# Four seven-product blocks and one plain unit in each feed-forward layer, in place of three and three

## The chip, the cores and the metric

The kernel runs on one NeuronCore of a Trainium2 chip. The metric is device time in microseconds (us) of one launch, from device measurement; the number before is the median of three runs. TensorE (PE) multiplies, VectorE (DVE), ScalarE (ACT) and GpSimd (POOL) prepare operands and read results, SyncE (SP) issues most of the transfers from device memory. [...]

## What is computed

An encoder trunk for 256 tokens of width 1024, two layers deep. Each layer is feed-forward, mixer, feed-forward, each with a residual and a layer norm; the mixer is an mLSTM in the first layer and a windowed attention in the second. The change touches the four feed-forward layers (FFNs):

```python
def swiglu(x, w_in, w_out):                 # x 256 x 1024, w_in 1024 x 5632, w_out 2816 x 1024
    gu = x @ w_in
    g, u = gu[..., :D_FF], gu[..., D_FF:]   # D_FF = 2816
    return (jax.nn.silu(g) * u) @ w_out

x = layer_norm(ALPHA * x + 0.5 * swiglu(x, ffn_w_in[l, 0], ffn_w_out[l, 0]), ...)
```

All of it is in 32-bit floats. TensorE multiplies a shorter format, so each operand is split into a high part (`_hi`, a rounded copy) and a low part (`_lo`, the operand less its high part), and one product is three matmuls: high by high, high by low, low by high (`mm3`).

## The kernel before

The weights are read once, in pieces ("words") of 128 x 1024 numbers, 512 KB each. The order in which the words are used is a list, the plan, made before anything is emitted. Each entry of the plan is one *split*: ACT writes `w_hi` (a cast), then DVE writes `w_lo` (a subtraction). At most `RING` = 10 splits exist ahead of TensorE. Raw words of kind `w_raw` have four buffers for the whole program and two more in an FFN (`v_raw`); words of kind `s_raw` have six buffers, which exist only inside an FFN and are opened at its start (`W.open`). All loads go through SP's queue in program order; transfers that add to what stands in SBUF go through POOL's.

The intermediate width 2816 of an FFN is worked off in blocks of columns:

- the **head**: 512 gate and 512 up columns by plain products, 8 splits, 96 matmuls of 128 x 512;
- then `GROUPS` = 3 times a **unit** and a **seven**. A unit is 256 gate and 256 up columns by plain products: 4 splits, 48 matmuls. A seven is 512 gate and 512 up columns by seven half-size products instead of eight (a Strassen-Winograd scheme): 14 splits, 84 matmuls instead of 96.

The seven takes x in four quarters (token half t, half of the 1024 inputs): A11, A12 for t = 0, A21, A22 for t = 1, and the weights in four quarters: B11, B21 (gate columns, upper and lower rows), B12, B22 (up columns). Each quarter of weights is two words. The products, named P1 to P7 here in the order of the plan, are

| product | x side | weight side | how the weight side is made |
|---|---|---|---|
| P1 | A11 | B11 | as loaded |
| P2 | A12 | B21 | as loaded |
| P3 | S1 = A21 - A22 | B11 + B12 | DVE adds, in place, after P1's split |
| P4 | S2 = S1 - A11 | + B22 | DVE adds, in place, after P3's split |
| P5 | S3 = A11 - A21 | B12 + B22 | DVE adds, in place |
| P6 | S4 = A12 + S2 | B22 | as loaded |
| P7 | A22 | P4's weights + B21 | transfer adds, in place, after P4's split |

So B11's two words are split three times with sums between the splits, and each such sum and split depends on the one before. The four sums of x, S1 to S4, are made and split once per FFN (`x_one`, `x_two`, `x_rest`); before the change they read `xr`, a copy of x that `x_raw` puts together from the high and low parts of the transposed x.

Between the products lie the **downs**, rows of `w_out` times finished columns of the hidden layer: `down(1)` is one split and 12 matmuls into four accumulators (`py`). A seven has four downs (after P2, P4, P6, P7; the last seven has two), a unit two, and six are left for the end (the tail), beside which the layer norm runs. Finished hidden columns are transposed by TensorE (`tr`), then split by ACT and DVE into `h_hi`, `h_lo`; `b_mul` makes the head's hidden columns `hh`.

A small model of the engines' clocks inside the program (`Paced`) decides where among the instructions the next cast, subtraction or sum is put. In the rows of the profile nearly every compute instruction has the line L134, since one helper records them all; groups are told apart by the names of their tiles: `w_lo<-s_raw` is a split of a seven's word, `w_lo<-w_raw` of any other word, `s_raw<-s_raw` a sum of weights by DVE, `S` and `S_lo` the sums of x, `py` matmuls are downs, `pw` matmuls everything else.

Of the kernel before, what the change touches and what calls it, by code (L numbers as in the profile page):

```python
# [12 lines left out]
OP = mybir.AluOpType  # L13
# [10 lines left out]
GROUPS = 3  # L24
# [292 lines left out]
def trunk_kernel(ctx: ExitStack, tc: tile.TileContext, x, ffn_w_in, ffn_w_out, ln_g, ln_b, ml_w_in, ml_gate_b,  # L317
# [42 lines left out]
    def seven(w, c0, c1, downs):  # L360

        at = lambda r0, c: [two(w, r0 + 256 * j, c) for j in range(2)]
        b12, b11, b22 = ([word(x, 2, "s_raw") for x in at(*p)] for p in ((0, c1), (0, c0), (512, c1)))
# [3 lines left out]
        for j in range(2):  # L367
            after[s1[j]] = [(b11[j], b12[j])]
        downs(0)
# [7 lines left out]
        [split_of(w_, None, p) for w_, p in zip(b12, s6)]  # L377
# [7 lines left out]
    for j, (kind, l, i, _) in enumerate(stages):  # L385
        if kind == "ffn":
# [112 lines left out]
    def to_xT(t, src, bank, halves=range(2)):  # L499
        for h in halves:  # L500
# [3 lines left out]
            split_evac(pair(xT, A, slice(4 * h, 4 * h + 4), tok(t)), p)  # L504

    def warm(n):

        p = ybank((128, 4, 128))
        for j in range(n):
            nc.tensor.transpose(p[:, j % 4], ident, ident)  # L510
# [64 lines left out]
    def ffn(l, i, n, pending, last):  # L575
        with ExitStack() as ph:
# [47 lines left out]
            xr = [pool.tile([128, 8, 128], F32, name=f"xr{t}", tag="h" + e, bufs=2) for t, e in enumerate(("_hi", "_lo"))]  # L624
            xs = {}
# [12 lines left out]
            low, high = slice(0, 4), slice(4, 8)  # L638
            f1 = {}
# [14 lines left out]
            if start:  # L654
                sg = {}
                for m in range(2):
                    ps = [wbank(), wbank()]
                    for a in range(4):
# [7 lines left out]
                        early = {2: lambda: x_raw(0), 3: lambda: x_raw(1), 4: x_one, 5: x_two, 6: x_rest}  # L666
# [7 lines left out]
            else:  # L674
                W.open(pool, ends[bound[0]])
                for t in range(2):
                    ps = [wbank(), wbank()]
                    for m in range(2):
                        for a in range(4):
# [5 lines left out]
                            if t == 1 and a % 2:  # L685
                                [[None, lambda: x_raw(0), None, lambda: x_raw(1)], [None, x_one, None, x_two]][m][a]()
# [675 lines left out]
```

## Time and profile before

| | |
|---|---|
| median of three runs | 942.7 us (942.70, 942.92, 941.75) |
| span of the profiled execution, first to last instruction | 941.2 us; no time of that execution beside its span is given, the three times lie 0.6 to 1.7 us above it |
| TensorE busy | 98% of the span, 4416 matmuls, granted clock 0.998 |
| VectorE busy | 85%, 943 instructions |
| ScalarE busy | 58% |
| GpSimd busy | 11% |
| transfers | 187.54 MB, mean 199 GB/s |

Order of the stages in the span: FFN 0 from the start to about 190 us, mLSTM, FFN 1 from about 300 us, FFN 2 from about 481 us, attention, FFN 3 from about 755 us. Busy shares are those of the profiler: the ends of matmuls are modelled, so the share of TensorE tells that it always has something in flight, not that it is at its peak; starts are exact.

### The profile page before, as it was taken

The numbers are of one execution on the slowest core, as the hardware profiler recorded it, in microseconds if no ns is written. First come the engines' busy times: TensorE is split into PE (matmuls) and PEld (weight loads), VectorE is DVE, ScalarE is ACT, GpSimd is POOL, SyncE is SP. The second block draws the span as 40 slices with busy tenths as digits, with TensorE's granted clock in tenths as the row PEclk, the third lists the DMA queues.
The fourth block names the chain that finished last, engine by engine and source line by source line (L and its number), as shares of the span: only waits on it lengthen the run. The fifth ranks groups of instructions, "written<-read, shape, count | busy, mean of one in ns | idle before, by whom it ended". The sixth has DMA issues, their size and how long they took to land.

```text
span 941.2 us, 12338 instructions
## 1 busy us (share of the span) xinstructions
PE 925.3 (98%) x4416; PEld 766.4 (81%) x4416; DVE 800.0 (85%) x943; ACT 546.5 (58%) x781; POOL 103.2 (11%) x162
## 2 busy tenths in 40 slices
PE   9999999999999999999999999999999999999996
PEld 7788888889878787888888888887887788888885
DVE  6899997787697889988888899977878888898975
ACT  5656756347563548565535566563678554757460
POOL 0030101011111000101010101010544300000100
PEclk9999999999999999999999999999999999999999
DMA  7969773646534949685549597746543266769531
GB/s 267 358 154 338 209 265 75 216 134 204 177 108 145 314 150 327 173 327 134 180 155 338 132 324 210 249 90 200 175 147 104 68 215 254 229 219 306 162 91 45
DMA packets 98461, 187.54 MB, mean 199 GB/s; under 512 B 6720, under 2 KB 37456, under 8 KB 98400
## 3 DMA queue, kind: packets, MB, share of 16 engines
q1 hardware_dynamic: 91072, 173.04, 53.1%
q0 software_dynamic: 6752, 12.66, 8.4%
q10 hardware_dynamic: 576, 1.05, 0.3%
q8 instruction: 35, 0.57, 0.2%
q14 instruction: 26, 0.21, 0.1%
HBM read 185.68 MB, written 1.05 MB: 198 GB/s over the span
## 4 chain that ended last, share of the span: by engine, by line
PE 73%; DVE 12%; DMA 6%; ACT 4%; issue 3%; POOL 1%; SPq 0%; DVEq 0%; ACTq 0%
PE pw L134 46%; PE py L134 27%; DVE w_lo L134 5%; DMA w_raw<-in_ffn_w_in_dram 3%; ACT w_hi L134 2%; DMA w_raw<-in_ffn_w_out_dram 1%; DVE s_raw L134 1%; DMA s_raw<-in_ffn_w_in_dram 1%; ACT sc L134 1%; DVE h L134 1%; DVE o L134 1%; DVE e L134 1%; DMA w_raw<-in_ml_w_in_dram 0%; DVE pr_lo L134 0%; ACT xT_hi L134 0%
## 5 line engine op out<-in xcount | busy, mean ns | idle before, releaser
L134 DVE TENSOR_TENSOR w_lo<-w_raw,w_hi 128x1024 fp32r<-128x1024 f32 (+1 forms) x237 | 280.9, 1216 | 16.0 <-ACT w_hi L134 14.0
L134 ACT CAST w_hi<-w_raw 128x1024 fp32r<-128x1024 f32 (+1 forms) x237 | 240.4, 1049 | 75.4 <-DMA w_raw<-in_ffn_w_out_dram 21.7
L134 PE MATMUL pw<-w_hi,xT_hi 128*128 128x512 f32 x560 | 222.6, 397 | 0.2 <-ACT xT_hi L134 0.2
L134 PE MATMUL pw<-w_hi,xT_lo 128*128 128x512 f32 x560 | 218.9, 391 | 0.2 <-DVE xT_lo L134 0.2
L134 PE MATMUL pw<-w_lo,xT_hi 128*128 128x512 f32 x560 | 218.3, 390 | 0.2 <-DVE w_lo L134 0.2
L134 ACT CAST w_hi<-s_raw 128x1024 fp32r<-128x1024 f32 x144 | 148.4, 1052 | 94.1 <-DVE s_raw L134 58.3
L134 DVE TENSOR_TENSOR w_lo<-s_raw,w_hi 128x1024 fp32r<-128x1024 f32 x144 | 172.6, 1219 | 19.2 <-ACT w_hi L134 19.1
L134 PE MATMUL py<-w_hi,h_hi 128*128 128x512 f32 x352 | 138.2, 393 | 0.3 <-ACT h_hi L134 0.3
L134 PE MATMUL py<-w_hi,h_lo 128*128 128x512 f32 x352 | 137.4, 390 | 0.2 <-DVE h_lo L134 0.2
L134 PE MATMUL py<-w_lo,h_hi 128*128 128x512 f32 x352 | 137.1, 390 | 0.2 <-DVE w_lo L134 0.2
L134 PEld LDWEIGHTS pw<-w_hi,xT_lo 128*128 128x128 f32 x560 | 105.1, 188 | 23.7 <-DVE xT_lo L134 1.0
L134 PEld LDWEIGHTS pw<-w_lo,xT_hi 128*128 128x128 f32 x560 | 105.4, 188 | 21.3 <-DVE w_lo L134 0.9
L134 PEld LDWEIGHTS pw<-w_hi,xT_hi 128*128 128x128 f32 x560 | 105.3, 188 | 21.0 <-ACT xT_hi L134 1.0
L134 DVE TENSOR_TENSOR s_raw<-s_raw 128x1024 f32<-128x1024 f32 x72 | 87.0, 1219 | 0.6
L263 POOL DMA_DIRECT2D s_raw<-in_ffn_w_in_dram x24 | 29.2, 1215 | 496.9 <-DVE w_lo L134 378.7
L134 PEld LDWEIGHTS py<-w_hi,h_lo 128*128 128x128 f32 x352 | 66.1, 188 | 15.2 <-DVE h_lo L134 1.4
L134 PEld LDWEIGHTS py<-w_lo,h_hi 128*128 128x128 f32 x352 | 66.1, 188 | 13.9 <-DVE w_lo L134 0.6
L134 PEld LDWEIGHTS py<-w_hi,h_hi 128*128 128x128 f32 x352 | 66.1, 188 | 13.9 <-ACT h_hi L134 0.7
L134 PE MATMUL pw<-w_hi,S_hi 128*128 128x512 f32 x192 | 74.7, 389 | 0.0
L134 PE MATMUL pw<-w_hi,S_lo 128*128 128x512 f32 x192 | 74.7, 389 | 0.0
L134 PE MATMUL pw<-w_lo,S_hi 128*128 128x512 f32 x192 | 74.7, 389 | 0.0
L134 DVE TENSOR_TENSOR h_lo<-pw,h_hi 128x512 fp32r<-128x512 f32 x44 | 30.1, 687 | 24.5 <-ACT h_hi L134 24.4
(218 smaller groups left out, 1118.1 us busy)
## 6 DMA issues: line engine op xcount, KB each, us to landing
w_raw<-in_ffn_w_out_dram SPq DMA_DIRECT2D x88, 512.0 KB, 5.3
s_raw<-in_ffn_w_in_dram SPq DMA_DIRECT2D x72, 512.0 KB, 6.1
w_raw<-in_ffn_w_in_dram SPq DMA_DIRECT2D x56, 512.0 KB, 5.2
w_raw<-in_ffn_w_in_dram SPq DMA_DIRECT2D x96, 256.0 KB, 4.7
s_raw<-in_ffn_w_in_dram POOLq DMA_DIRECT2D x24, 512.0 KB, 6.1
w_raw<-in_ml_w_in_dram SPq DMA_DIRECT2D x24, 512.0 KB, 4.6
w_raw<-in_at_w_in_dram SPq DMA_DIRECT2D x12, 512.0 KB, 3.8
w_raw<-in_ml_w_out_dram SPq DMA_DIRECT2D x8, 512.0 KB, 3.8
```

What stands on the lines that cost most here:

```text
L134: r = f(out, *args, **kw)
L263: nc.gpsimd.dma_start(t.rearrange("p (k f) -> p k f", k=self.words[w]["k"]), v, accum_op=OP.add)
```

## The change

Each FFN becomes: head, seven, seven, unit, seven, seven, tail. The order is now a list, `PARTS`, with the number of downs at each place; the first three sevens have four downs, the last has two, the unit has two and the tail six, as before. Three further edits come with it. The second of the two words of B12 + B22 (P5's weights) gets its B22 by an adding transfer from device memory (`BY_DMA = (1,)`), issued after the first sum, instead of by DVE. The sums of x read the transposed x where TensorE left it in PSUM (`xp`), and one quarter, A21, is first copied to SBUF by ACT (`x_copy`); `xr` and `x_raw` are gone, and in FFNs 1 to 3 all of the sums now come inside the head. The list of words has B11 ahead of B12. `warm` takes its PSUM bank from the other pool.

```diff
-GROUPS = 3
+PARTS = [("s", (1, 1, 1, 1)), ("s", (1, 1, 1, 1)), ("u", 2), ("s", (1, 1, 1, 1)), ("s", (1, 1, 0, 0))]
+TAIL = 6
+BY_DMA = (1,)
...
     def seven(w, c0, c1, downs):
-        b12, b11, b22 = ([word(x, 2, "s_raw") for x in at(*p)] for p in ((0, c1), (0, c0), (512, c1)))
+        b11, b12, b22 = ([word(x, 2, "s_raw") for x in at(*p)] for p in ((0, c0), (0, c1), (512, c1)))
...
-        for j in range(2):
+        t3 = [None, None]
+        for j, a in enumerate(at(512, c1)):
             after[s1[j]] = [(b11[j], b12[j])]
+            if j in BY_DMA:
+                after[s1[j]].append((b12[j], a))
+                t3[j] = s1[j]
...
         for j, a in enumerate(at(512, c0)):
-            after[s6[j]] = [(b11[j], a), (b12[j], b22[j])]
+            after[s6[j]] = [(b11[j], a)]
+            if j not in BY_DMA:
+                after[s6[j]].append((b12[j], b22[j]))
+                t3[j] = s6[j]
...
-            for g in range(GROUPS):
-                c0 = 512 + 768 * g
-                for a in range(4):
-                    beside(wi, a * 256, c0, F + c0)
-                down(2)
-                seven(wi, c0 + 256, F + c0 + 256, lambda i_: down(1) if g < GROUPS - 1 or i_ < 2 else None)
-            down(6)
+            c0 = 512
+            for what, n_ in PARTS:
+                if what == "u":
+                    for a in range(4):
+                        beside(wi, a * 256, c0, F + c0)
+                    down(n_)
+                    c0 += 256
+                else:
+                    seven(wi, c0, F + c0, lambda i_, n_=n_: down(n_[i_]))
+                    c0 += 512
+            down(TAIL)
...
             split_evac(pair(xT, A, slice(4 * h, 4 * h + 4), tok(t)), p)
+            xp[t, h] = p
...
-            def x_raw(t):
-                nc.vector.tensor_add(xr[t], xT[0][:, :, tok(t)].bitcast(F32), xT[1][:, :, tok(t)].bitcast(F32))
...
+            def x_copy():
+                f1["a21"] = temp("a21").rearrange("p (k m) -> p k m", k=4)
+                nc.scalar.copy(f1["a21"], xp[1, 0])
             def x_one():
-                f1["S1"] = x_sum("S1", xr[1][:, low], OP.subtract, xr[1][:, high])
+                f1["S1"] = x_sum("S1", f1["a21"], OP.subtract, xp[1, 1])
             def x_two():
-                f1["S2"] = x_sum("S2", f1["S1"], OP.subtract, xr[0][:, low])
+                f1["S2"] = x_sum("S2", f1["S1"], OP.subtract, xp[0, 0])
             def x_rest():
-                x_sum("S4", xr[0][:, high], OP.add, f1["S2"])
-                x_sum("S3", xr[0][:, low], OP.subtract, xr[1][:, low])
+                x_sum("S3", xp[0, 0], OP.subtract, f1["a21"])
+                x_sum("S4", xp[0, 1], OP.add, f1["S2"])
...
-                                [[None, lambda: x_raw(0), None, lambda: x_raw(1)], [None, x_one, None, x_two]][m][a]()
+                                [[None, x_copy, None, x_one], [None, x_two, None, x_rest]][m][a]()
...
-                if g == 0 and not start:
-                    x_rest()
-                turn = seven(g < GROUPS - 1, unit_turn)
+            turns = [lambda t=t: tr(hB0, t, hs[t]) for t in range(0 if start else 1, 2)]
+            for g, (what, n_) in enumerate(PARTS):
+                if what == "u":
+                    turns = [unit(turns)]
+                    down(n_)
+                else:
+                    turns = [seven(n_, turns)]
```

In the changed program TensorE has 4368 matmuls instead of 4416, and POOL issues 48 adding transfers of 512 KB instead of 24. The transposes of the head's last hidden columns, which stood in the middle of the first unit, stand right behind P1 of the first seven.

More of the change, by code (lines that the diff above doesn't have):

```diff
@@ L722, in copied, with seven @@
                 return e
-            def seven(full, unit_turn):
+            def seven(downs, turns):
                 of = lambda k0, t: (lambda k: pair(xT, A, k0 + k, tok(t)))
@@ L758, in seven @@
                 product(qa, of(0, 0), True, end1)
-                unit_turn()
+                for f in turns:
+                    f()
                 product(qc, of(4, 0), True, end2)
-                down(1)
+                down(downs[0])
                 qb = wbank()
@@ L764, in seven, with unit @@
                 product(qa, sum_("S2"), False, end6)
-                down(1)
+                down(downs[1])
                 product(qa, sum_("S3"), False, end7)
                 product(qb, sum_("S4"), False, end3)
-                if full:
-                    down(1)
+                if downs[2]:
+                    down(downs[2])
                     tr(hB, 0, v["u0"])
                 product(qa, of(4, 1), False, end4)
-                if full:
-                    down(1)
-                else:
+                if not downs[2]:
                     tr(hB, 0, v["u0"])
+                down(downs[3])
                 return lambda: tr(hB, 1, v["u1"])
-            turn = None
-            for g in range(GROUPS):
+            def unit(turns):
                 ps = [wbank(), wbank()]
@@ L788, in ffn @@
                     if a == 1:
[L789 to L793 removed]
+                        for f in turns:
+                            f()
                 hh = []
```

28 lines of the change are left out of this document (11 added, 17 removed).

## The prediction

> **What bounds the kernel now.** I read the page first: the span, then busy time and the transfer queues.
>
> ```profile
> span 941.2 us, 12338 instructions
> ...
> PE 925.3 (98%) x4416; PEld 766.4 (81%) x4416; DVE 800.0 (85%) x943; ACT 546.5 (58%) x781; POOL 103.2 (11%) x162
> ...
> q1 hardware_dynamic: 91072, 173.04, 53.1%
> q0 software_dynamic: 6752, 12.66, 8.4%
> ...
> s_raw<-in_ffn_w_in_dram POOLq DMA_DIRECT2D x24, 512.0 KB, 6.1
> w_raw<-in_ml_w_in_dram SPq DMA_DIRECT2D x24, 512.0 KB, 4.6
> ```
>
> TensorE is busy 98% of the span, VectorE 85%. The waits of TensorE, longest first, then tell whether the 98% hides starvation:
>
> ```profile
> PE py L134 <- DVE ident L134: 1.4, 1, 1.4
> ```
>
> The longest wait in total is 1.4 us. So TensorE sets the time, and a matmul that goes is a gain in full, provided that the split weights still come in time. What one costs is read from the chain of waits in order of time, in the steady part of FFN 2 (start, length, what):
>
> ```profile
> 515.79 5.44 PE py L134 x24
> ...
> 535.30 2.72 PE py L134 x12
> ...
> 563.49 5.44 PE py L134 x24
> ```
>
> 24 matmuls take 5.44 us, 226.7 ns each. The rows at 515.79 and 563.49 are both the downs of a unit, so 47.7 us is one unit and one seven. The table by stretches has VectorE's share of that period:
>
> ```profile
> 515.79:563.49 47.70, 47.70 (x218) 39.39 (x217) 43.94 (x46) 30.50 (x38) 2.42 (x2) 1.00 0.72 226
> ```
>
> VectorE works 43.94 of 47.70 us: it is the next bound, 8% behind. Its groups in two such periods (count, then busy us and mean ns):
>
> ```profile
> L134 DVE TENSOR_TENSOR s_raw<-s_raw 128x1024 f32<-128x1024 f32 x16 | 19.4, 1220 | 0.2
> L134 DVE TENSOR_TENSOR h_lo<-pw,h_hi 128x512 fp32r<-128x512 f32 x6 | 4.1, 686 | 0.7 <-ACT h_hi L134 0.7
> L134 DVE TENSOR_TENSOR e<-e,pw 128x512 f32<-128x512 f32 x4 | 2.7, 680 | 0.0
> ```
>
> **The steady balance.** Back to back, a DVE instruction on 1024 columns takes less than its 1.22 us: starts lie 1.14 us apart (503.80 and 504.94 below). By the same difference an instruction on 512 takes 0.61. A seven with four downs is 84 + 48 matmuls, 29.9 us, and eight transposes, about 0.9 us: 30.8 us. For it VectorE now does 18 splits, 6 sums, 5 steps on products and 2 `h_lo`: 24 x 1.14 + 7 x 0.61 = 31.6 us. A unit with two downs is 72 matmuls and four transposes, 16.8 us; VectorE needs 6 x 1.14 + 0.75 + 0.61 = 8.2 us. So VectorE falls a little behind in every seven and earns 8 us in every unit, and today a unit stands ahead of each seven.
>
> **The change part by part.**
>
> *Matmuls.* Per FFN two units (96) go and one seven (84) comes: 12 fewer, 48 in all, 48 x 0.2267 = 10.9 us less. Transposes and downs stay in number. This is the whole gain, as TensorE is the bound: 942.7 - 10.9 = 931.8 if nothing waits.
>
> *VectorE's work.* Per FFN six splits come (6.8 us), 20 sums stand where 18 did (2.3), two `x_raw` additions go (2.3), steps on products and `h_lo` grow by about 1.5: 8 us more per FFN, 800 to about 833 us. A mean of 87% isn't a bound; the order is.
>
> *Half of P5's sum by transfer.* One DVE sum per seven goes: 30.5 us instead of 31.6, just under TensorE's 30.8. POOL issues 24 more adding transfers; its row gives 6.1 us to landing. The transfer starts after the first two sums, P5's second split comes six splits and four sums later, about 11 us, so 5 us of cover. POOL's queue holds behind it only the next such transfers and, in FFN 0, small loads for the mLSTM. Cost nothing; if a landing came 5 us later than that, TensorE would wait for the excess.
>
> *Sums of x from PSUM.* Two DVE additions (2.3 us) go, one ACT copy of 512 columns comes, on an engine 58% busy. The steps read PSUM at 680 ns (`e<-e,pw`) and SBUF at 680 (the `S` row below): no price. [...] The four `py` banks are held until the last sum; the first down comes after P2, later than that sum, so nothing waits for the banks.
>
> *The start of each FFN.* Here I expect the loss. In FFN 2 of the trace (start, length; DVE):
>
> ```profile
> 487.84 1.22 DVE L134 TENSOR_TENSOR w_lo<-w_raw,w_hi 128x1024 fp32r<-128x1024 f32 x1
> ...
> 503.80 1.23 DVE L134 TENSOR_TENSOR w_lo<-s_raw,w_hi 128x1024 fp32r<-128x1024 f32 x1 [0.52 <-ACT w_hi L134]
> 504.94 0.68 DVE L134 TENSOR_TENSOR S<-xr 128x512 f32<-128x512 f32 x1
> 506.31 0.69 DVE L134 TENSOR_TENSOR S_lo<-S,S_hi 128x512 fp32r<-128x512 f32 x1 [0.69 <-ACT S_hi L134]
> ...
> 517.31 0.75 DVE L134 TENSOR_TENSOR hh<-sg,pw 128x256 f32<-128x256 f32 x2 [0.32 <-ACT sg L134]
> ...
> 531.70 1.22 DVE L134 TENSOR_TENSOR w_lo<-w_raw,w_hi 128x1024 fp32r<-128x1024 f32 x1
> ```
>
> The first split of P1 ends at 505.02 (503.80 + 1.22); the split of the down after P4 ends at 532.92. VectorE takes 27.9 us for that stretch. It holds all four sums of x, each with a 0.69 us wait for ACT's cast, and for the unit only the `hh` pair (0.75 + 0.32 idle) and one `h_lo` with its wait, about 0.9. Without the unit it is 26 us. TensorE's way over the same stretch is from 521.23 (515.79 + 5.44) to 535.30: 14.1 us. So VectorE must have P1's first split 12 us ahead of its use. Today it has 16, since unit and downs lie between. After the change P1 follows the head at once. The head ends where the unit's first matmul starts:
>
> ```profile
> 504.28 0.39 PE L134 MATMUL pw<-w_hi,xT_hi 128*128 128x512 f32 x1
> ```
>
> At 504.3 + 14.1 = 518.4 TensorE would want the down after P4. When can VectorE have it? The loads decide, in SP's order:
>
> ```profile
> 489.08 1.20 SPq L98 DMA_DIRECT2D w_raw<-in_ffn_w_in_dram  x2
> 491.42 1.48 SPq L100 DMA_DIRECT2D w_raw<-in_ffn_w_out_dram  x2
> 493.00 2.86 SPq L100 DMA_DIRECT2D s_raw<-in_ffn_w_in_dram  x4
> ```
>
> ```profile
> DMA to landing us min/median/max: 6.9/9.1/11.3
> ```
>
> A seven's words are loaded behind the second of the first two downs' words, and in the changed program too. That one waits for a `w_raw` buffer, which the head's eighth split frees (487.84 + 1.22 = 489.06); the unit's words at 489.08 and one more `w_raw` are no longer ahead. So B11 is asked for at about 489.6 instead of 493.0. If its landing takes the 6.9 us of the quickest one in this stretch, it is there at 496.5; with the 4.6 us of the page's last row above, loads of the same size with less ahead of them, at 494.2. The split itself, a cast about as long as the subtraction's 1.22 and the subtraction, adds 2.3, so P1's first split ends between 496.5 and 498.8, and the down after P4 is split 26 us later, 522.5 to 524.8. TensorE waits 4.1 to 6.4 us in this FFN. I take 4.6, near the lower end, since fewer loads are queued ahead than in the trace. Part of it should stand behind P1, where the transposes of `hh` wait: `hh` now follows all sums of x on DVE's queue.
>
> FFN 3 has the same order: 4.6 us. FFN 1 too, with slower loads at its start:
>
> ```profile
> 312.99 7.68 DMA s_raw<-in_ffn_w_in_dram
> ```
>
> 7.7 us instead of 6.9: I take 4.6 here too. FFN 0 makes the sums of x earlier:
>
> ```profile
> 26.61 2.35 DVE L134 TENSOR_TENSOR w_lo<-w_raw,w_hi 128x1024 fp32r<-128x1024 f32 x2
> ...
> 42.89 1.22 DVE L134 TENSOR_TENSOR w_lo<-s_raw,w_hi 128x1024 fp32r<-128x1024 f32 x1
> ...
> 62.59 1.22 DVE L134 TENSOR_TENSOR w_lo<-w_raw,w_hi 128x1024 fp32r<-128x1024 f32 x1
> ```
>
> ```profile
> 31.19 0.39 PE L134 MATMUL pw<-w_hi,xT_hi 128*128 128x512 f32 x1
> ```
>
> There the stretch takes 63.81 - 44.11 = 19.7 us, and P1's first split can't come before the head's eighth split (about 27.8, the first of the pair at 26.61), two remaining sums of x (4 x 0.61 + 2 x 0.69), one `hh` and itself: 33.4. So the down after P4 is split at 53 or later; TensorE wants it at 31.2 + 14.1 + 0.4 = 45.7, a wait of 7.4. I take 6.4, since without `x_raw` the eighth split may come earlier; if the remaining sums too are done before it, 3.8 us go and 2.6 are left.
>
> *The second seven.* It follows without a unit. At 30.5 against 30.8 us VectorE gains nothing on it, and inside a seven it needs its lead, since the sums fall between P1 and P5. I take 1 us per FFN, between 0 and 2.5. From the unit on VectorE has some 8 us of lead, and the rest runs as now.
>
> **The sum.** 4.6 x 3 + 6.4 + 4 x 1 = 24.2 us of waits, less 10.9: 13.3 us more. On the profiled span 941.2 becomes 954.5; the median lies 1.5 us above the span, so 956. With the low ends (4.1 x 3 + 2.6 + 0) it is 947, with the high ends (6.4 x 3 + 7.4 + 10) 968; hardly all at once, so 947 to 966 for this case.
>
> **Rivals.**
>
> *The lead holds: faster.* If B11 lands early enough for P1's first split to be done by 492.4 (518.4 - 26) in FFN 2 and correspondingly elsewhere, TensorE never waits, and the time is 931.8. It breaks even at 2.7 us of waits per FFN, a split done by 495.1. For it: the six `s_raw` buffers are free early and SP could ask sooner than I think; VectorE's 26 us holds waits that shrink when it is late. Against: the landing rows, and that today's lead of 16.2 us at P1 (505.02 against 521.23) is down to 2.4 at the down after P4 (532.92 against 535.30). 931.8 to 941, chance 0.22. That it comes out within 0.2% (about 2 us, what a measurement of this kernel can tell from no change) is the edge between the cases: 0.05.
>
> *Transfers become the bound: slower still.* By the queue rows a 512 KB load takes 53.1% of 941.2 us over 330 such loads, 1.51 us of all 16 engines, and an adding transfer 8.4% over 24, 3.3 us. Two sevens need 24 of the one and 6 of the other, 56 us, against 61.6 of TensorE. If the adding ones grew by half when three fall in one seven, it would be 66, 4 us over in each FFN: 956 + 17 = 973. [...] Against: today's share stays at 0.72 in the steady period above, and words are asked for 10 us ahead. Chance 0.07.
>
> **How the numbers follow.** Forecast 956, chance 0.66. Slower in all 0.66 + 0.07 = 0.73, same 0.05, faster 0.22. The range reaches down into the faster case to 936, leaving about 0.1 below, and up to 966, leaving 0.09 above.
>
> **What the profile after would show.** Right: 4368 matmuls; VectorE near 830 us busy; waits of TensorE for `w_lo`, `h_lo` or the transposed `hh` of several us in each of the four first sevens, none after the unit; the stretch from P1 to the down after P4 some 5 us longer than 14.1. Wrong: TensorE's starts without gaps there (then the loads came earlier, or VectorE needed less than 26 us), or gaps in the third and fourth sevens (then the balance of the unit is wrong).

## The result, and the profile after

| | us, median | ratio to before (95% interval) |
|---|---|---|
| before (run beside it) | 942.33 | |
| after | 1005.93 | 1.0674 (1.0655 to 1.0694) |
| forecast | 956, 936 to 966 | |

The change costs 63.6 us; 13 were forecast. The page of the kernel after, by the same lines as before:

```profile
span 1003.0 us, 12342 instructions
...
PE 937.7 (93%) x4368; PEld 764.2 (76%) x4368; DVE 836.1 (83%) x971; ACT 576.0 (57%) x813; POOL 132.3 (13%) x186
...
q1 hardware_dynamic: 82368, 173.04, 48.9%
q0 software_dynamic: 13280, 25.25, 15.4%
...
s_raw<-in_ffn_w_in_dram POOLq DMA_DIRECT2D x48, 512.0 KB, 6.0
```

The work is as forecast: 4368 matmuls and VectorE 836 us busy (forecast some 830). But TensorE is busy 93% instead of 98%. Its waits, longest in total first (us in total, times, longest):

```profile
PE pw L136 <- DVE w_lo L136: 18.5, 22, 2.2
PE pw L136 <- DVE hh L136: 18.3, 3, 9.0
PE py L136 <- DVE w_lo L136: 7.8, 8, 1.8
PE py L136 <- DVE h_lo L136: 4.9, 3, 2.0
```

Before, the longest total here was 1.4 us. In every one of these rows TensorE waits for VectorE. Where, the table by stretches tells. These are the blocks of FFN 2, each from its first matmul to the next block's: head, first seven, second seven, unit, third seven, fourth seven, tail. (Columns: length; busy us and count of PE, PEld, DVE, ACT and POOL; granted clock; share and rate of transfers.)

```profile
513.46:537.90 24.44, 23.72 (x109) 19.09 (x108) 17.74 (x22) 11.65 (x16) 1.46 (x1) 1.00 0.83 296
537.90:577.30 39.40, 33.41 (x141) 26.44 (x140) 34.03 (x37) 23.17 (x28) 3.64 (x3) 0.96 0.60 176
577.30:610.33 33.03, 31.63 (x141) 25.40 (x140) 30.85 (x31) 21.24 (x25) 3.62 (x3) 1.00 0.85 244
610.33:627.14 16.81, 16.81 (x77) 13.90 (x76) 15.78 (x16) 9.87 (x12) 1.20 (x1) 1.00 0.83 286
627.14:658.02 30.88, 30.88 (x141) 25.55 (x140) 28.79 (x30) 19.78 (x24) 2.41 (x2) 1.00 0.82 244
658.02:684.76 26.74, 25.68 (x117) 20.97 (x116) 19.47 (x19) 16.02 (x19) 3.61 (x3) 1.00 0.53 124
684.76:708.49 23.73, 20.03 (x85) 15.52 (x84) 20.39 (x24) 9.97 (x13) 1.46 (x1) 0.93 0.51 177
```

The last seven and the tail of FFN 2 in the kernel before:

```profile
616.66:642.08 25.42, 25.42 (x117) 21.06 (x116) 20.68 (x21) 18.10 (x21) 1.20 (x1) 1.00 0.52 135
642.08:660.68 18.60, 18.31 (x85) 14.57 (x84) 13.12 (x18) 4.94 (x8) 1.46 (x1) 1.00 0.54 178
```

A seven at full pace takes 30.9 us, the last one 25.4, as they did before; a unit takes 16.8. The unit and the third seven run at full pace, the first seven takes 8.5 us more, the second 2.2, the fourth 1.3, and the tail 5.1 more than the 18.6 of before. The other layers, from starts read in the same way:

| us more than full pace (tail and head: than before) | FFN 0 | FFN 1 | FFN 2 | FFN 3 | sum | forecast |
|---|---|---|---|---|---|---|
| head | 2.5 | -0.7 | 1.2 | 0.3 | 3.3 | with the next |
| first seven | 5.3 | 11.3 | 8.5 | 8.7 | 33.8 | 20.2 |
| second seven | 3.3 | 2.2 | 2.2 | 2.1 | 9.8 | 4 |
| unit, third seven | 0 | 0 | 0 | 0 | 0 | 0 |
| fourth seven and tail | 6.9 | 9.1 | 6.4 | 5.4 | 27.8 | 0 |

74.7 us in all, less 10.9 of matmuls and less 2.7 that the blocks of before had lost themselves, is 61.1; the spans differ by 61.8.

**The first seven.** TensorE in FFN 2 (start, length, what, and in brackets the wait before it and for whom):

```profile
545.19 1.09 PE L136 MATMUL pw<-ident,hh 128*128 128x128 f32 x4 [4.63 <-DVE hh L136]
...
546.51 0.63 PE L136 MATMUL pw<-w_lo,xT_hi 128*128 128x512 f32 x1
546.93 0.63 PE L136 MATMUL pw<-w_hi,xT_lo 128*128 128x512 f32 x1
```

```profile
545.10:548.00 2.90, 2.81 (x9) 2.46 (x10) 2.15 (x3) 1.53 (x2) 0.00 (x0) 0.50 0.00 0
548.00:551.00 3.00, 3.00 (x13) 2.42 (x13) 1.68 (x3) 1.05 (x1) 1.21 (x1) 0.95 0.00 0
```

After P1 TensorE stands for 4.63 us until `hh` is there, and then works at about half pace: matmuls start 0.42 us apart instead of 0.23. The second view, by stretches, says why: the clock granted from 545.1 to 548.0 is 0.50. VectorE in the same stretch:

```profile
528.61 0.69 DVE L136 TENSOR_TENSOR xT_lo<-py,xT_hi 128x512 fp32r<-128x512 f32 x1 [3.91 <-ACT xT_hi L136]
...
529.82 2.35 DVE L136 TENSOR_TENSOR w_lo<-s_raw,w_hi 128x1024 fp32r<-128x1024 f32 x2
...
558.88 1.22 DVE L136 TENSOR_TENSOR w_lo<-w_raw,w_hi 128x1024 fp32r<-128x1024 f32 x1
```

P1's first split ends at 531.04 (the first of the pair at 529.82), the split of the down after P4 at 560.10 (558.88 + 1.22). That is 29.1 us where I had reckoned 26. The row at 528.61 is `xT_lo`, which waited 3.91 us for ScalarE and stands ahead of that split. ScalarE was late with its `xT_hi` (done at 528.58) because the cast of B11's first word stands ahead of it and waited for its load:

```profile
527.05 1.05 ACT L136 CAST w_hi<-s_raw 128x1024 fp32r<-128x1024 f32 x1 [3.07 <-DMA s_raw<-in_ffn_w_in_dram]
```

So the late landing of B11 delays P1's split twice, by the word itself and by `xT_lo`. B11's loads on SP's queue (start, time in which they were issued, count):

```profile
517.18 4.42 SPq L102 DMA_DIRECT2D w_raw<-in_ffn_w_out_dram  x2
522.51 3.38 SPq L102 DMA_DIRECT2D s_raw<-in_ffn_w_in_dram  x6
```

The loads of two downs, which wait for buffers, take until 521.60; the seven's words follow at 522.51, 9.05 us after the layer's first matmul.

**The end.** VectorE and TensorE at P7's second word and in the tail of FFN 2:

```profile
677.50 0.69 DVE L136 TENSOR_TENSOR e<-e,pw 128x512 f32<-128x512 f32 x1 [2.13 <-PE pw L136]
680.22 0.69 DVE L136 TENSOR_TENSOR e<-pw,e 128x512 f32<-128x512 f32 x1 [2.03 <-PE pw L136]
...
681.56 1.22 DVE L136 TENSOR_TENSOR w_lo<-s_raw,w_hi 128x1024 fp32r<-128x1024 f32 x1
```

```profile
682.83 0.50 PE L136 MATMUL pw<-w_lo,xT_hi 128*128 128x512 f32 x1 [1.06 <-DVE w_lo L136]
...
687.40 0.49 PE L136 MATMUL py<-w_lo,h_hi 128*128 128x512 f32 x1 [1.77 <-DVE w_lo L136]
...
700.89 0.50 PE L136 MATMUL py<-w_hi,h_lo 128*128 128x512 f32 x1 [1.75 <-DVE h_lo L136]
```

The split of P7's second word (681.56) stands behind three steps on products, and the first two wait 2.13 and 2.03 us for TensorE. It is ready at 682.78, TensorE uses it at 682.83: its lead, the time for which a split is ready before TensorE uses it, is down to 0.05 us. From there the tail's words come one by one, just in time, and then this follows on ScalarE:

```profile
692.43 1.05 ACT L136 CAST w_hi<-w_raw 128x1024 fp32r<-128x1024 f32 x1 [4.23 <-DMA w_raw<-in_at_w_in_dram]
...
697.57 0.58 ACT L136 CAST h_hi<-pw 128x512 fp32r<-128x512 f32 x1
```

The cast `h_hi` of the last seven's second half stands in ScalarE's queue behind the casts of the attention's first words, which wait for their loads, 4.23 us ahead of the first. Those were issued from 688.54 on; that they went out no sooner because the tail's late splits gave their buffers free late is a reading that no run takes apart. `h_hi` is done at 698.15. Its `h_lo` then stands in VectorE's queue as well, behind splits of the same attention words (695.05 to 698.92) and two steps of the layer norm:

```profile
700.16 0.67 DVE L136 TENSOR_TENSOR h_lo<-pw,h_hi 128x512 fp32r<-128x512 f32 x1
```

TensorE needs this `h_lo` at 699.1, and it is done at 700.83 (the row at 700.89 above is TensorE's next matmul).

### The profile page after: what moved, and what is told of

Its sections match the earlier page's. It is cut to its first block, busy times and chain, and to the rows that moved or that the text cites. A ratio compares the mean times of both kernels' runs of the same rounds, so it can differ in the third digit from the quotient of the medians.

```text
span 1003.0 us, 12342 instructions
## 1 busy us (share of the span) xinstructions
PE 937.7 (93%) x4368; PEld 764.2 (76%) x4368; DVE 836.1 (83%) x971; ACT 576.0 (57%) x813; POOL 132.3 (13%) x186
## 3 DMA queue, kind: packets, MB, share of 16 engines
q1 hardware_dynamic: 82368, 173.04, 48.9%
q0 software_dynamic: 13280, 25.25, 15.4%
## 4 chain that ended last, share of the span: by engine, by line
PE 59%; DVE 21%; DMA 7%; ACT 6%; issue 5%; POOL 1%; SPq 1%; DVEq 0%; ACTq 0%; POOLq 0%
PE pw L136 38%; PE py L136 21%; DVE w_lo L136 10%; DMA s_raw<-in_ffn_w_in_dram 4%; ACT w_hi L136 2%; DVE s_raw L136 2%; DVE x L136 1%; DVE h_lo L136 1%; DMA w_raw<-in_ffn_w_in_dram 1%; DVE e L136 1%; ACT sc L136 1%; ACT S_hi L136 1%; DVE S L136 1%; DVE S_lo L136 1%; SPq L102 1%
## 5 line engine op out<-in xcount | busy, mean ns | idle before, releaser
L136 DVE TENSOR_TENSOR w_lo<-w_raw,w_hi 128x1024 fp32r<-128x1024 f32 (+1 forms) x213 | 252.9, 1216 | 16.9 <-ACT w_hi L136 15.5
L136 ACT CAST w_hi<-s_raw 128x1024 fp32r<-128x1024 f32 x192 | 196.4, 1050 | 105.3 <-DVE s_raw L136 58.1
L136 DVE TENSOR_TENSOR w_lo<-s_raw,w_hi 128x1024 fp32r<-128x1024 f32 x192 | 229.8, 1219 | 24.4 <-ACT w_hi L136 23.9
L136 ACT CAST w_hi<-w_raw 128x1024 fp32r<-128x1024 f32 (+1 forms) x213 | 215.0, 1047 | 34.3 <-DMA w_raw<-in_ffn_w_in_dram 8.7
L136 PE MATMUL pw<-w_lo,xT_hi 128*128 128x512 f32 x480 | 189.5, 395 | 6.5 <-DVE w_lo L136 6.5
L136 PE MATMUL pw<-w_hi,xT_hi 128*128 128x512 f32 x480 | 193.6, 403 | 1.1 <-ACT xT_hi L136 1.1
L136 PE MATMUL pw<-w_hi,xT_lo 128*128 128x512 f32 x480 | 189.0, 394 | 0.0
L265 POOL DMA_DIRECT2D s_raw<-in_ffn_w_in_dram x48 | 58.1, 1210 | 536.5 <-DVE s_raw L136 156.6
L136 PE MATMUL pw<-w_lo,S_hi 128*128 128x512 f32 x256 | 102.0, 398 | 12.1 <-DVE w_lo L136 12.0
L136 PEld LDWEIGHTS pw<-w_lo,S_hi 128*128 128x128 f32 x256 | 48.0, 188 | 30.1 <-DVE w_lo L136 20.9
```

What stands on the lines that cost most here:

```text
L136: r = f(out, *args, **kw)
L265: nc.gpsimd.dma_start(t.rearrange("p (k f) -> p k f", k=self.words[w]["k"]), v, accum_op=OP.add)
```

## The experiments

18 kernels. "After" is the changed kernel; u and s stand for unit and seven. All are timed beside the kernel before, whose median was 941.8 to 942.9.

| | order | us | ratio (95%) |
|---|---|---|---|
| e1 | u s u s u s | 957.8 | 1.0155 to 1.0185 |
| e2 | s s s u s | 989.8 | 1.0494 to 1.0526 |
| e3 S3, S4 later | as after | 999.8 | 1.0584 to 1.0629 |
| e4 sums on VectorE | as after | 1010.0 | 1.0662 to 1.0739 |
| e5 `ADDING` 3000 | as after | 1013.0 | 1.0724 to 1.0784 |
| e6 loads from POOL | as after | 1016.7 | 1.0762 to 1.0813 |
| e7 e6 and e3 | as after | 1010.9 | 1.0701 to 1.0751 |
| e8 no sums of x | as after | 987.3 | 1.0457 to 1.0492 |
| e9 | u s s s s | 995.2 | 1.0540 to 1.0580 |
| e10 e1 and S3, S4 later | u s u s u s | 953.6 | 1.0101 to 1.0138 |
| e11 e1, sums on VectorE | u s u s u s | 948.2 | 1.0048 to 1.0078 |
| e12 e10, `ADDING` 5000 | u s u s u s | 942.2 | 0.9987 to 1.0011 |
| e13 S3, S4 later, `ADDING` 3000 | u s s s s | 985.2 | 1.0432 to 1.0478 |
| e14 e10, sums on VectorE | u s u s u s | 947.1 | 1.0036 to 1.0068 |
| e15 e13's order and sums of x, sums on VectorE | u s s s s | 986.6 | 1.0446 to 1.0486 |
| e16 e13, both sums by transfer | u s s s s | 995.7 | 1.0516 to 1.0568 |
| e17 transposes in the wait | as after | 1001.0 | 1.0584 to 1.0628 |
| e18 e16, tail of four | u s s s s | 1002.4 | 1.0574 to 1.0668 |

### Is it the order of the blocks? (e1, e2, e9)

```diff
 e1: PARTS = [("u", 2), ("s", (1, 1, 1, 1)), ("u", 2), ("s", (1, 1, 1, 1)), ("u", 2), ("s", (1, 1, 0, 0))]
 e2: PARTS = [("s", (1, 1, 1, 1)), ("s", (1, 1, 1, 1)), ("s", (1, 1, 1, 1)), ("u", 2), ("s", (1, 1, 0, 0))]
 e9: PARTS = [("u", 2), ("s", (1, 1, 1, 1)), ("s", (1, 1, 1, 1)), ("s", (1, 1, 1, 1)), ("s", (1, 1, 0, 0))]
```

> The changed kernel with the blocks again in the order unit, seven, unit, seven, unit, seven; the sums of x from PSUM and the adding transfer for half of P5's sum stay. Theory (the order of the blocks is the cause): about 942 us, 938 to 946, as the kernel before, with no wait of TensorE over 1.5 us in the four layers. Rival (the sums of x from PSUM, or the transfers, cost the time): 955 us or more, with the waits for hh still there.

> The changed kernel with the unit ahead of the last seven (seven, seven, seven, unit, seven). Theory (the end of each layer loses because the last seven follows a seven and so starts with too little lead to cover the transfer for P7's second word): the 28 us that the last seven and the tail lose in the four layers go, the third seven now loses some 2 us per layer: about 985 us, and the tails are again under 19 us long in FFN 0 to 2. Rival (the end loses because of the transfers themselves or because of the start): 1000 us or more, the tails still 23 us or longer.

> The changed kernel with the unit ahead of the first seven (unit, seven, seven, seven, seven). Theory (a seven needs some 5.5 us of VectorE's lead at its start; a unit earns 8, a seven leaves 3): no seven of 36 us or more any more, the second, third and fourth each 2 us too long, the ends as lossy as in the changed kernel: 984 us, 978 to 990. Rival (the sums of x and the loads at the start cost it wherever the unit stands): the unit or the first seven 5 us or more too long, 1000 us or more.

Mostly, but not alone. With three and three again, 957.8: some 48 of the 64 us go, 16 stay, so the theory's 938 to 946 was missed and the rival's 955 was reached. e2 bears out what it was made for: with a unit ahead of it the last seven of FFN 2 is at full pace and the tail takes 18.92 us, against 18.60 before, at the cost of a third seven of 33.1 us:

```profile
600.67:633.80 33.13, 31.76 (x142) 25.33 (x141) 31.83 (x32) 21.43 (x25) 3.61 (x3) 1.00 0.86 242
...
650.61:676.00 25.39, 25.39 (x117) 21.06 (x116) 22.41 (x23) 17.00 (x21) 2.41 (x2) 1.00 0.53 111
676.00:694.92 18.92, 18.29 (x85) 14.57 (x84) 15.31 (x20) 7.27 (x10) 1.46 (x1) 1.00 0.70 234
```

In all four layers the last sevens and tails of e2 lose 2.3 us of the 27.8. Its time, 989.8, is still 5 us above the 985 that stood for it, and FFN 1's tail, 19.3 us, just misses the forecast of under 19.

In e9 no first block loses over 2.4 us, and the sevens that follow a seven take 33.0 to 33.9, as expected; the time, 995.2, is 5 us above the range, since FFN 1's first seven takes 32.1 and the fourth sevens 29 instead of 26.7. So in these orders, with `ADDING` at 8000, a seven without a unit ahead of it loses wherever it stands, and the last one draws the tail with it; e13 below has two such sevens that do not lose.

### The 16 us that stay with three and three (e10, e11, e14, e12)

They lie in one place above all, FFN 1: its three sevens take 32.05, 32.11 and 26.88 us, its tail 25.4 instead of 18.3. VectorE in e1, first seven of FFN 1:

```profile
361.61 0.69 DVE L136 TENSOR_TENSOR e<-e,pw 128x512 f32<-128x512 f32 x1 [4.36 <-PE pw L136]
364.40 0.69 DVE L136 TENSOR_TENSOR e<-pw,e 128x512 f32<-128x512 f32 x1 [2.10 <-PE pw L136]
...
368.11 0.69 DVE L136 TENSOR_TENSOR h_lo<-pw,h_hi 128x512 fp32r<-128x512 f32 x1 [2.22 <-ACT h_hi L136]
368.71 1.22 DVE L136 TENSOR_TENSOR w_lo<-s_raw,w_hi 128x1024 fp32r<-128x1024 f32 x1
```

and ScalarE's cast of the last of these words, P7's second:

```profile
357.18 1.04 ACT L136 CAST w_hi<-s_raw 128x1024 fp32r<-128x1024 f32 x1
```

The word has been cast by 358.22, VectorE has nothing else to do, and still its split starts at 368.71: three steps on products and an `h_lo` stand ahead of it, and VectorE waits 4.36 and 2.10 us for TensorE and 2.22 for a cast that follows TensorE's transposes. The lead at this word is thrown away, the next unit earns it back, and the next seven throws it away again. The program's own model of the clocks chose this order; it counts on 8 us (`ADDING`) for an adding transfer. The runs that take the two edits out one by one, and change that constant:

```diff
 e10 (as e3, in FFN 1 to 3):
-[None, x_two, None, x_rest]]
+[None, x_two, None, lambda: None]]
...
+            if not start:
+                turns.append(x_rest)
 e11: BY_DMA = ()
 e14: both
 e12: e10 and ADDING = 5000.0
```

> The order unit, seven three times with the other edits (957.8 us) and S3 and S4 behind the transposes of hh in FFN 1 to 3. Theory (in that kernel hh stands behind four sums on VectorE, and the lead it loses in FFN 1 is never earned back): the first units of FFN 2 and 3 lose their 1.9 us, FFN 1's sevens are no longer 32 us: 940 to 948 us. Rival (the adding transfers take the lead): 953 us or more.

> The order unit, seven three times with the other edits (957.8 us), but all of P5's sums on VectorE. Theory (the sums of x ahead of hh cost the 16 us): 955 us or more, since VectorE has 1.14 us more to do in each seven. Rival (the adding transfer for half of P5's sum costs them): 940 to 946 us.

> Unit, seven three times, S3 and S4 later, and all of P5's sums on VectorE: of the change only the sums of x from PSUM remain. Theory (the 16 us of the kernel with three and three come from the place of S3 and S4 and from the order that the adding transfer brings, one by one): 942 us, 939 to 944. Rival (reading x from PSUM costs by itself): 946 us or more.

> The kernel with unit, seven three times and S3, S4 later (953.6 us), with the program's own estimate of an adding transfer at 5 us instead of 8 (ADDING = 5000). In FFN 1 this leaves 3, 1 and 2 steps on products ahead of the split of P7's second word on VectorE's queue, instead of 4, 4 and 3. Theory (those steps wait for TensorE, and so VectorE's lead is thrown away there): FFN 1's second and third sevens and its tail lose nothing any more, 944 us, 940 to 947. Rival (the adding transfers themselves cost the 10 us): 950 us or more.

S3 and S4 ahead of `hh` cost 4 us (957.8 to 953.6), and FFN 1's sevens stayed at 32.1. Without the extra transfers the same kernel takes 948.2, FFN 1's tail 18.3 again: both edits have a share. The forecast for e10 fell to its rival, and e11 lies between its two. e12 settles which share is whose: transfers, sums from PSUM and amounts of work all as in e10, only the model's constant differs (which moves other choices of the model too), and the 11 us go. Its page:

```profile
span 939.9 us, 12427 instructions
...
PE 923.9 (98%) x4416; PEld 765.8 (81%) x4416; DVE 779.8 (83%) x923; ACT 548.7 (58%) x785; POOL 116.9 (12%) x174
```

So in this order of blocks neither reading x from PSUM nor the adding transfers cost anything by themselves: with them VectorE is 20 us less busy than before (780 against 800), and the time is that of before, 942.2, within 0.12%. e14 missed its 939 to 944, and its rival can't be the reason, as e12 reads the same x from PSUM. In e14 S3 and S4 fall into a seven with one more sum on VectorE, and the first sevens of FFN 2 and 3 take 32.6 and 32.1; that the one causes the other is a reading, which no run tests.

### The start (e3, e8, e17, e6, e7)

e3 is the changed kernel with the edit of `x_rest` shown with e10.

> The changed kernel with x_rest (S3 and S4) put behind the transposes of hh in FFN 1 to 3, so that hh does not stand behind them on VectorE. Theory (hh waits only since it stands behind the sums, and TensorE's clock halves after waits of over 4 us): the waits for hh (18.3 us in three layers) fall to under 5, the half clock at that place goes, some of it comes back as waits for w_lo: about 990 us. Rival (VectorE's sum of work between P1 and the down after P4 sets the time, in whatever order): within 5 us of 1006.

The waits for `hh` fell from 18.3 to 5.4 us and the granted clock was 1.00 in the first sevens of FFN 2 and 3, which still take 37.1 us instead of 39.4: of the 12.9 us that went there, 5.8 came back as waits for `w_lo` (22.7 and 9.4 us in the two rows instead of 18.5 and 7.8). 999.8 lies between the two, 1 us outside the rival's range: the place of S3 and S4 in VectorE's queue is the smaller part, and what it has to do in that stretch the larger, as e8 shows.

```diff
 e8: in x_sum nothing is made; P3 to P6 read quarters of xT
 e17:
+                turns.insert(0, lambda: warm(84 if bound[0] == 2 else 44, nc.nc))
```

> The changed kernel without the sums of x: S1 to S4 are not made, and P3 to P6 take quarters of x as they stand (so the result of these products is another one; all transfers, sums of weights, splits and matmuls stay). It takes eight VectorE steps of 0.61 us and four waits of 0.69 us for ScalarE, some 7.7 us, out of the start of each layer. Theory (VectorE's amount of work between P1 and the down after P4 decides): the first sevens of FFN 2 and 3 fall from 39.4 to 32.5 us or less, that of FFN 1 by 8: about 975 us. Rival (the late landing of B11 decides): first sevens of 37 us or more, 995 us or more.

The first sevens of FFN 2 and 3 fell to 32.5 and 32.5, as the theory said; B11 was asked for as late as ever, 9.06 us after the first matmul of FFN 2, so the rival falls there. P1's first split came hardly sooner either, 17.3 us after the layer's first matmul (17.6 in after), while VectorE's stretch from it to the split of the down after P4 fell from 29.1 to 18.3 us. The total, 987.3, lies between the two, since FFN 1's first seven fell only from 42.1 to 39.2 and the second sevens grew to 34.3: what the first no longer lost, the next lost in part.

> The changed kernel with 84 (FFN 1) or 44 (FFN 2 and 3) transposes of a constant, whose results nobody reads, between P1 and the transposes of hh in the first seven, so that TensorE is busy during its waits for hh (9.0, 4.6 and 4.7 us). No engine's order is changed else. Theory (a wait of over 4 us is followed by some 3 us at a granted clock of 0.5): the granted clock stays at 1.00 there, the first sevens are 1.5 to 2 us shorter, 1001 us, 999 to 1003. Rival (the slow restart has another cause, or VectorE's lateness swallows it): 1005 us or more.

```profile
536.42:543.60 7.18, 7.18 (x55) 6.71 (x54) 5.12 (x9) 2.35 (x4) 0.00 (x0) 1.00 0.28 94
543.60:546.60 3.00, 3.00 (x18) 2.58 (x17) 2.75 (x3) 1.53 (x2) 0.00 (x0) 1.00 0.00 0
```

1001.0, as the theory said. These are P1's last matmuls with the added transposes, and the 3 us behind them, in FFN 2: what had a clock of 0.50 has 1.00. The first sevens are 1.2, 1.4 and 1.6 us shorter, 4.2 in all. The medians differ by 4.9, but other blocks that the edit does not touch differ too: FFN 1's tail is 1.4 us shorter and FFN 0 1.5 longer. So some 4 to 5 of the 64 us are the halved clock behind three waits. VectorE's own waits for TensorE shrink with it: in the stretch from P1's split to the down after P4 of FFN 2 two of them are 0.25 and 0.31 us instead of 0.76 and 1.32.

```diff
 e6: in W.open
-        self.load()
+        self.load(engine=self.nc.gpsimd)     # the six s_raw loads from POOL's queue
...
+            for _ in range(2):
+                pool.tile([128, D], F32, name="skip", tag="s_raw", bufs=S_RAW)
             gb = load_ln(...)
 e7: e6 and e3
```

> The changed kernel with the first six loads of a seven's words in each layer issued from POOL instead of from SP, where they stand behind two loads of downs that wait for buffers, and with ln_g and ln_b two buffers further on, so that the first words of the next layer need not wait for the layer norm. Theory (P1's first split is late because B11 is asked for late): VectorE's 5.65 us wait ahead of that split in FFN 1 goes, the first seven gains 5 us or more there and 2 to 4 in FFN 2 and 3: 992 to 998 us. Rival (VectorE's work in that stretch sets the time, whenever B11 lands): 1003 to 1008 us.

> The loads of the run before and, in FFN 1 to 3, S3 and S4 behind the transposes of hh. Theory: both causes of the late start are gone but VectorE's amount of work in the stretch, the first sevens take 34 us or less instead of 36 to 42: about 983 us. Rival (the amount of work is what decides): 996 us or more, as with S3 and S4 moved alone.

Both missed their theories (e7 lies in its rival's range, e6 in neither), because the edit did not do what it was meant to. In FFN 2 the loads went out no sooner (527.80, 9.6 us after the layer's first matmul, against 9.05 after), since they wait for the layer norm of the stage before whichever buffers `ln_g` and `ln_b` have; six from POOL then landed 7.5 to 10.4 us after issue instead of 4.5 to 8.7. And on ScalarE:

```profile
527.80 4.40 POOL L97 DMA_DIRECT2D s_raw<-in_ffn_w_in_dram  x6 [2.56 <-DVE x L136]
```

```profile
535.30 1.04 ACT L136 CAST w_hi<-s_raw 128x1024 fp32r<-128x1024 f32 x1 [6.58 <-DMA s_raw<-in_ffn_w_in_dram]
536.26 0.58 ACT L136 CAST xT_hi<-py 128x512 fp32r<-128x512 f32 x1
```

The cast of B11 stands in ScalarE's queue ahead of the second half of `xT_hi` and holds it for 6.58 us, and TensorE's head with it (29.5 us instead of 24.4). In FFN 1 the loads did go out 2.1 us sooner, and the first seven gained 0.7. What B11's landing alone is worth stays open by these two.

### The end, and sevens that follow sevens (e4, e5, e13, e15, e16, e18)

```diff
 e4:  BY_DMA = ()
 e5:  ADDING = 3000.0
 e13: PARTS of e9, x_rest as in e10, ADDING = 3000.0
 e15: PARTS of e9, x_rest as in e10, BY_DMA = ()
 e16: e13 and BY_DMA = (0, 1)
 e18: e16, the last seven ("s", (1, 1, 1, 1)), TAIL = 4
```

> The changed kernel with all sums for P5 on VectorE again (24 adding transfers instead of 48). Theory (VectorE's lead is what lacks): 24 more sums of 1.14 us on VectorE, 1008 to 1020 us, with longer waits for w_lo in the second seven of each layer. Rival (the adding transfers are the bound): under 1000 us.

> The changed kernel with one constant of the model of the clocks inside the program altered: it now counts on an adding transfer after 3 us instead of 8 us (ADDING = 3000), which in the last seven puts the split of P7's second word and the tail's first split ahead of the two steps that read the product bank of P6 instead of behind them. Nothing else changes. Theory (the end loses since that split stands on VectorE's queue behind steps that wait for TensorE): the 28 us that the last seven and the tail lose in the four layers fall under 10, about 985 us. Rival (the adding transfer itself, 8.7 us from issue to landing there, is what ends last): the split comes no sooner, 1003 us or more.

e4's time is in the theory's range, 1010.0, with an interval that overlaps that of after: fewer adding transfers (32, two for each of 16 sevens, against 48) don't help. But the longer waits for `w_lo` that the theory wanted did not come: 13.4 and 6.2 us in the two rows instead of 18.5 and 7.8. The first sevens took 0.6 to 1.1 us longer than in after, the second ones at most 0.9. In e5 the fourth sevens do return to 25.4 us, but the first sevens grow by 1.2 to 2.2 us and the tails to 26.4 to 27.7 in FFN 0 to 2: the casts of the tail's and the next stage's words have moved ahead too, `h_hi` waits behind them (6.7 us in all), and the sum is 1013.0. So the place of P7's split is worth 1.3 us per layer in the fourth seven. That the tail's 4 to 8 us come from words that are late altogether is a reading, which no run tests apart from the order of the queue. Of the orders with four sevens only e2, where a unit gives the lead, removed them, but for 2.3 us.

> The kernel with the unit first, then four sevens (995.2 us), with S3, S4 later and ADDING = 3000, which leaves one step on products instead of three ahead of the split of P7's second word in most sevens. Theory (VectorE's amount of work would do; lead is thrown away in that queue): sevens that follow a seven take under 31.6 us instead of 33.1, and the tails under 22: 945 to 965 us. Rival (VectorE's amount of work in a seven is what lacks): 33 us again, 982 us or more.

> The kernel with the unit first, S3, S4 later, and all of P5's sums on VectorE, so 31.6 us of VectorE's time in a seven against 30.8 of TensorE's. Theory (the amount of work matters little beside the lead thrown away in the queue): within 8 us of the same order with the adding transfers and ADDING = 8000, which took 995.2 us. Rival (the amount decides): each of three sevens 1 us longer still, over 1003 us.

e13's time, 985.2, is the rival's; of the theory's sevens only two came, the second ones of FFN 2 and 3, which run at full pace (30.88 instead of 33.1). Those of FFN 0 and 1 take 33.9 and 32.2, the third ones 33.5 to 34.7, and the fourth and the tails lose as ever. P1's first split of the four sevens of FFN 2 is ready 14.4, 9.6, 4.8 and 4.0 us ahead of its use. VectorE between these splits:

```profile
567.17:602.83 35.66, 35.66 (x164) 29.51 (x163) 32.17 (x34) 21.35 (x27) 3.65 (x3) 1.00 0.82 241
```

From P1's split of the second seven to that of the third it needs 35.66 us, 32.17 of them busy and 3.5 idle, where TensorE needs 30.88. The groups of that stretch name most of the idle time: 2.7 us wait for `w_hi`.

```profile
L136 DVE TENSOR_TENSOR w_lo<-s_raw,w_hi 128x1024 fp32r<-128x1024 f32 x13 | 15.4, 1220 | 2.7 <-ACT w_hi L136 2.7
```

They are two waits, 1.77 us at P5's words and 0.88 at P6's. Their casts stand on ScalarE behind copies of products, and the first of these waits for TensorE:

```profile
588.07 0.59 ACT L136 COPY e<-pw 128x512 f32<-128x512 f32 x1 [4.64 <-PE pw L136]
```

So these waits come from a queue as well: VectorE waits for ScalarE, and ScalarE for TensorE. The adding transfers have no part in them: the one into P5's second word was issued at 577.08, and none of this stretch took over 9.5 us to landing.

e15, with one sum more on VectorE in place of a transfer, is as fast (986.6), 8.6 us below the 995.2 that stood for it, 0.6 more than its theory allowed; the rival's 1003 falls. But its third sevens take 34.0 us in all four layers against 33.0 to 33.2 in e9, the 1 us that the rival named, while its second sevens are shorter than e9's. e15 differs from e9 in the place of S3 and S4 as well, and from e13 in `ADDING`, so what the amount of work (1.14 us more per seven) is worth stays open.

> The kernel with the unit first, S3, S4 later and ADDING = 3000 (985.2 us), now with both halves of P5's sum by adding transfer, so one sum of 1.14 us less on VectorE in each seven. Theory (from one seven to the next VectorE's lead falls by some 4.8 us, partly by its amount of work, partly by its own waits in its queue): the fall is 3.6 us, the third sevens take under 32 us, the fourth still wait: 960 to 975 us. Rival (72 adding transfers instead of 48 are too many for the transfer engines): 985 us or more.

> The run with both halves by transfer, and in the last seven four downs instead of two, with four instead of six left for the tail. Theory (the fourth seven loses because its lead is used up; downs cost TensorE 2.72 us and VectorE 1.14, so two of them give it 3 us back ahead of P7 and the tail's splits come in time): 4 us or more under the run without it. Rival (fewer downs behind the last products leave the layer norm uncovered): longer than that run.

By their times the rivals won both. e16 has 64 adding transfers, four for each of 16 sevens; they take 7.8 us to landing instead of 6.1, and a new wait leads its list, for steps on products that stand behind splits of words still being added:

```profile
s_raw<-in_ffn_w_in_dram POOLq DMA_DIRECT2D x64, 512.0 KB, 7.8
```

```profile
PE pw L136 <- DVE e L136: 19.0, 10, 4.4
```

e18 has a wait of 22.1 us for `h_hi` in its tails, so its rival's reason, an uncovered layer norm, is not shown. No version of four sevens came below 985, and none of all below the kernel before by more than the interval.

## Why the prediction was wrong

The sign was right, and the mechanism of the start and of the second seven; the sizes were not, and one step was wrong outright.

*Matmuls, -10.9.* Right: 4368, and blocks at full pace are as long as before. *VectorE near 830 us.* Right, 836.

*The start, 4.6 us in FFN 1 to 3 and 6.4 in FFN 0.* Right in place, mis-sized: 33.8 instead of 20.2, and 3.3 more in the heads. In FFN 2 the terms can be followed. "P1's first split ends between 496.5 and 498.8": in the time of the kernel before (its FFN 2 starts 32.18 us earlier) it ended at 498.9, the upper end, 1.9 us later than the value I took. B11 landed in 4.52 us, quicker than I had reckoned, but was asked for 0.7 us later, and the split stood behind the late `xT_lo`. "Without the unit it is 26 us": it was 29.1, 3.1 more, for VectorE itself waits when TensorE is late: in FFN 2 0.28 and 0.76 us for `h_hi` and 1.32 for P2's bank, and an `h_lo` of the head (0.6) falls into the stretch. About 1.5 of it is the halved clock at second hand, as e17's 0.25 and 0.31 us at two of these waits tell. 4.6 + 1.9 + 3.1, less the head's own delay of 1.2, is 8.4 of the 8.5 measured. I had named that effect ("waits that shrink when it is late") with the wrong sign. In the other layers I carried 4.6 over; FFN 1, where VectorE stood idle for 5.7 us ahead of B11 with all sums of x queued behind, lost 11.3.

*"Part of it should stand behind P1, where the transposes of `hh` wait".* Right, 18.3 us; not foreseen, that the granted clock was 0.50 to 0.52 behind these waits of 9.04, 4.63 and 4.64 us (e17: some 4 to 5 us in all).

*The second seven, 1 us, 0 to 2.5.* Right in place, above the range: 2.1 to 3.3. A seven needs its lead inside; one that starts with 3 us of it waits for P4's words, by 2.2 us. e13 shows what I had left out of 30.5 against 30.8: VectorE's own waits, some 3.5 us in a seven.

*"From the unit on VectorE has some 8 us of lead, and the rest runs as now."* This is the step that failed, at 27.8 us. The unit and the third seven did run as before; the fourth seven of FFN 2 started with 11 us of lead where its like had 18 before. That is too little, as e2 shows, which removed all but 2.3 us of the loss with a unit at that place; which part of it is the order in which P7's second word and the tail are queued, and which words that come late anyway, stays open.

*Half of P5's sum by transfer: nothing; sums of x from PSUM: no price.* As operations, right: a sum of x takes 678 to 684 ns from PSUM in the kernel after, 682 to 686 from `xr` before, and e12, which has both edits with three and three, takes 942.2 us, as the kernel before. As entries in fixed queues, wrong: in e1 they cost 16 us, about 4 by the place of S3 and S4 and about 11 by the order that the model chose around the adding transfers.

*The rivals.* "The lead holds" fell with P1's first split at 498.9 against the 495.1 it needed. "Transfers become the bound" fell too: 173 MB and 25 MB take a share of 48.9% and 15.4%, an adding transfer lands after 6.0 us as before (6.1), and e4, with fewer, was no faster.

## What to carry to other kernels

Where two engines are balanced within a few per cent, count the lead of the feeding engine from block to block, at each place where it dips, and include its own waits on the other: VectorE, once late, waited more here, not less (29.1 us for a stretch that I had reckoned at 26), and in the tail of FFN 2 `h_hi` stood behind a wait of 4.23 us for a word of the next stage. A split whose word is ready but which stands behind a step that waits for the consumer throws the lead away (in e1 the word was cast by 358.22 and split from 368.71), so look at the order in the queue before the amount of work. Two edits that are free by their operations can still cost a per cent by where they land in the queue (957.8 us in e1, 942.2 in e12).

## What the runs showed of the hardware

In the kernel after, the wait of TensorE of 4.63 us in FFN 2 was followed by some 3 us at half its pace: 0.50 granted from 545.1 to 548.0. Behind the waits of 9.04 and 4.64 us in FFN 1 and 3 it was 0.50 from 349.45 to 352.3 and 0.52 from 834.94 to 837.8. A stretch of short waits ended so as well: in the tail of FFN 2, with gaps of 1.77 us and less, TensorE was busy for 1.47 of 3.24 us, and the clock then fell to 0.57.

```profile
684.76:688.00 3.24, 1.47 (x7) 0.86 (x5) 3.08 (x4) 3.24 (x5) 0.00 (x0) 1.00 0.00 0
688.00:692.00 4.00, 3.83 (x11) 2.68 (x10) 3.89 (x4) 0.20 (x1) 0.00 (x0) 0.57 0.45 159
```

But the same tail in e17, a run in which no down waited over 2.0 us, went on at 1.00, with TensorE busy for 19.46 of 23.84 us, and took as long (23.73 us in the kernel after). So short waits did not halve the clock in each run, and what decides it stays open. e17 also shows that useless work in the wait kept the clock up: 44 or 84 transposes filled it, and the granted clock in these first sevens was 1.00.
